# Tap tables of 32 rows, the order at the start of the second block, and the pooling gate on the unscaled input

## The chip, the cores and the metric

The kernel runs on one core of one Trainium2 chip. The metric is the device time in microseconds (us) of one execution; the median of several runs counts. A profile of one execution stands beside it. Engine names: TensorE (PE in the rows, PEld for its weight loads), VectorE (DVE), ScalarE (ACT), GpSimd (POOL) and SyncE (SP), whose queue issues most of the DMAs.

## The reference, cut to what matters

The reference runs two blocks on a sequence of 256 tokens of width 1024, in float32. The first block (a hybrid mixer, a cross attention and a large sum over 16384 experts) ends in an RMS norm. The second block has two layers, each fed by a modulated RMS norm; the first has a convolution mixer with 31 taps, the second a pooling mixer.

```python
def _rms(x, g):
    y = x * lax.rsqrt(jnp.mean(x * x, axis=-1, keepdims=True) + EPS)
    return y * g

# in each layer i of the second block
sh, sc, gt = jnp.split((silu(c) @ w_mod[i] + b_mod[i])[:, None, :], 3, axis=-1)
h = _rms(x, norm_g[i]) * (1.0 + sc) + sh
x = x + gt * o                      # o: the mixer's output for h

def _conv_mixer(h, w_in, dw, db, ln_g, ln_b, w_out):
    a, b, g = jnp.split(h @ w_in, 3, axis=-1)
    y = a * sigmoid(b)
    y = depthwise_conv(y, dw) + db          # 31 taps, centred
    return (silu(_layernorm(y, ln_g, ln_b)) * silu(g)) @ w_out

def _pool_mixer(h, w_in, w_grp, scale, w_out):
    v, g = jnp.split(h @ w_in, 2, axis=-1)
    pooled = windowed_means(v, (2, 4, 8, 16)) - v
    y = grouped_matmul(pooled, w_grp) * scale
    return (y * silu(g)) @ w_out
```

## The kernel before

Activations lie as eight slices of 128 channels by 256 tokens (`h[:, k, :]`). Every weight tile of 128 x 1024 comes from memory as `raw`, is split by ScalarE into a rounded part `hi` (line 142) and by VectorE into the rest `lo` (line 144), and is used in three matmuls for each slice (hi with the high part of the input, hi with its low part, lo with the high part). Three `raw` buffers and, in the main ring, three pairs of `hi` and `lo` are in turn; `load_next` issues the loads on SP's queue, and `take` and `split_next` run ahead of the matmuls. A tile scheduler that simulates the engines sets the final order on each engine; `issue_after(x)` in the code holds the instructions of x's engine behind x, and an order by program text decides among those that are ready.

The last stages, which the change touches:

- `peer_down` (lines 1263 to 1265) multiplies the 128 expert tiles `V` into the sums `y`. Beside it runs `second_prep`, which loads the tables of the second block: `rcnt`, `fwd`, then `ftap` and `dw` (lines 1343 to 1346, 31 rows each: one row for a tap), and `inv`, all on SP's queue between the loads of expert tiles.
- `last_pair` and `first_out` finish the first block: for each pair p of slices, VectorE adds `y` to `h`, ScalarE squares it, and TensorE adds the squares into one row sum `s2` (line 1298, two matmuls for a pair, each in two passes since the operands are plain float32).
- `second` begins with the modulated norm of the first layer. VectorE and ScalarE make `v2` and `rho` (lines 1408 to 1412), an inverse root of `s2`; `mod_input` then makes the input `xa` of the conv mixer slice by slice: `mi` = h * gain * rho on VectorE (line 1384), `xah` = mi + shift, rounded, on ScalarE (line 1386), and `xal`, what the rounding left, on VectorE (line 1387).
- The taps enter as a transfer function: `ftap` (taps by frequency) times `dw` (taps by channel) gives `wf` in eight float32 matmuls of 512 columns (line 1422, two passes each), copied out by ScalarE (line 1423). Tables m = 0 go to the PSUM pool `psM`, the six others to the four buffers of `psT`.
- `x0_gen` makes the block's own input, the first block's final norm, in `h`: a column sum `cs` on TensorE, an inverse root `r1` (lines 240 and 241 on VectorE), and eight products (line 1431).
- `natural` (lines 212 to 214) then multiplies `xa` by the weights of a and b of the conv mixer; `b_evac` joins a pair by Tanh (`th`) and a product, and goes on to the convolution by transforms.
- The output of the conv mixer is added to `h` in `out_evac`. It also makes `f`, two tiles of the gain times `h` (high and low part) with the shift of the second layer in two further columns (258 columns), while the mean square is still being summed; when it is there, line 1604 makes `r`, and line 1605 the scaled input `xa` by another `mod_input`.
- The values of the pooling mixer are made from `f` (lines 1649 to 1651), into pairs of `psT` buffers; `from_gain` then multiplies by r (VectorE) and adds the shift's column as a bias (ScalarE). The gate is made from `xa` by `pair` (lines 155 to 157), into the two buffers of `psM`, and `silu_gate` takes its Silu on ScalarE (line 1392). The pooling itself (`pooled`: adds, means, splits) is VectorE's, between the splits of the weights.
- The grouped matmuls (`mmg`, line 1680) and the product with the gate (`yg`) follow, also in `psM`, and then the output matmul.

Of the kernel before, what the change touches and what calls it, by code (L numbers as in the profile page):

```python
# [6 lines left out]
F32 = mybir.dt.float32  # L7
# [3 lines left out]
AF = mybir.ActivationFunctionType  # L11
OP = mybir.AluOpType
AX = mybir.AxisListType

T = 256
D = 1024
KB = 8
EPS = 1e-6
CW = 31
WINDOWS = (2, 4, 8, 16)  # L20
NF = 272
NC = NF // 2 - 127
# [18 lines left out]
class Net:  # L41
# [1245 lines left out]
    def first_out(self, p):  # L1287

        post, V, A, P = self.post1, self.V, self.A, self.P
        if p == 0:  # L1290
            self.s2 = self.psX.tile([128, 512], F32, tag="x", name="s2")[:, 0:T]
        hp = self.h[:, 2 * p:2 * p + 2, :]
        V.tensor_add(hp, self.y[p], hp)
        sq = post.tile([128, 2, T], F32, tag="sq2", bufs=2, name="sq2")
        A.activation(sq, hp, AF.Square)
        for i in range(2):
            k = 2 * p + i
            P.matmul(self.s2, lhsT=self.gf2[:, k, :], rhs=sq[:, i, :], start=(k == 0), stop=(k == KB - 1))
        if p == 0:
            self.sq0 = sq  # L1300
        elif p == 1:
            self.acc2 = post.tile([128, 2, T], F32, tag="rawc", name="acc2")
            V.tensor_add(self.acc2, self.sq0, sq)
        else:
            V.tensor_add(self.acc2, self.acc2, sq)
# [25 lines left out]
    def second_prep(self):  # L1331

        nc, I, pool = self.nc, self.I, self.post1
        V, A, G, P = self.V, self.A, self.G, self.P
        mod = self.mod
        xa = self.xa2 = self.newx(pool, "xa")
        self.rcnt = pool.tile([128, 4, T], F32, name="rcnt")
        nc.sync.dma_start(self.rcnt, I["rcnt"])
        yield from self.pause(8)
        f = pool.tile([128, 2, 4, 128], F32, tag="rawc", name="fwd")  # L1340
        nc.sync.dma_start(f, I["fwd"])
        yield from self.pause(8)
        self.ftap = pool.tile([CW, 4, 128], F32, name="ftap")
        nc.sync.dma_start(self.ftap, I["ftap"])
        self.dw = pool.tile([CW, D], F32, name="dw")
        nc.sync.dma_start(self.dw, I["cv_dw"])
        yield
        om = self.om = pool.tile([128, 128], F32, name="om")
        G.memset(om, 1.0 / 768)
        g2 = pool.tile([128, 8], F32, name="g2")  # L1350
        gf = self.col("norm_final", 0, 8)
        V.tensor_mul(g2, gf, gf)
        V.tensor_scalar(g2, g2, 1.0 / D, EPS / D, op0=OP.mult, op1=OP.add)
        self.gf2 = pool.tile([128, KB, 128], F32, name="gf2")
        G.tensor_copy(self.gf2, g2.unsqueeze(2).to_broadcast([128, KB, 128]))
        yield
        self.fh = pool.tile([128, 2, 4, 128], F32R, name="fh")
        self.fl = pool.tile([128, 2, 4, 128], F32R, name="fl")
        A.activation(self.fh, f, AF.Copy)
        V.tensor_sub(self.fl, f, self.fh.bitcast(F32))  # L1360
        yield
        inv = pool.tile([128, 3, T], F32, tag="rawc", name="inv")
        nc.sync.dma_start(inv, I["inv"])
        yield from self.pause(8)
        self.ih = pool.tile([128, 3, T], F32R, name="ih")
        self.il = pool.tile([128, 3, T], F32R, name="il")
        self.ln_exp(A.activation(self.ih, inv, AF.Copy))
        V.tensor_sub(self.il, inv, self.ih.bitcast(F32))
        yield
        while "mod" not in self.flags:  # L1370
            yield
        mv = mod.rearrange("p (l c) -> p l c", l=2)
        mg = self.mg = pool.tile([128, 2, 8], F32, name="mg")
        V.scalar_tensor_tensor(mg, mv[:, :, 8:16], 1.0, self.col("norm_g", 0, 16).rearrange("p (l c) -> p l c", l=2),
                               op0=OP.add, op1=OP.mult)
        V.tensor_mul(mg[:, 0, :], mg[:, 0, :], self.col("norm_final", 0, 8))
# [10 lines left out]
            i = self.V.scalar_tensor_tensor(xl[:, k, :], t, sh, xh[:, k, :].bitcast(F32), op0=OP.add, op1=OP.subtract)  # L1387
        return i

    def silu_gate(self, ps, p):  # L1390

        self.A.activation(self.sg[:, 2 * p:2 * p + 2, :], ps, AF.Silu)
        yield

    def second(self):
        nc, I, post = self.nc, self.I, self.post
        V, A, G, P = self.V, self.A, self.G, self.P
        h, mod = self.h, self.mod
        xa = self.xa2
# [4 lines left out]
        acc, s2 = self.acc2, self.s2  # L1404


        v2 = post.tile([128, T], F32, name="v2")
        V.tensor_scalar(v2, s2, EPS * EPS, None, op0=OP.add)
        rho = post.tile([128, T], F32, name="rho")
        A.activation(rho, v2, AF.Ln)  # L1410
        A.activation(rho, rho, AF.Exp, scale=-0.5)
        self.rsqrt2(post, v2, rho)
        done = self.mod_input(0, xa, rho)

        wf = [post.tile([128, 2, D], F32, tag=f"big{i}", name="wf") for i in range(2)]
        for m in range(4):
            for c in range(2):
                if m:
                    ps = self.psT.tile([128, 512], F32, tag="t", name="wfp")
                else:  # L1420
                    ps = self.psM.tile([128, 512], F32, tag="mm", name="wfm")
                P.matmul(ps, lhsT=self.ftap[:, m, :], rhs=self.dw[:, c * 512:(c + 1) * 512], start=True, stop=True)
                A.activation(wf[m // 2][:, m % 2, c * 512:(c + 1) * 512], ps, AF.Copy)

        def x0_gen():
            s1 = self.colsum(acc)
            with self.tc.issue_after(done.ins):
                v1, r1 = self.rsqrt1(post, s1, 1.0 / D, [128, T], "r1")
            self.rsqrt2(post, v1, r1)
            for k in range(KB):  # L1430
                V.scalar_tensor_tensor(h[:, k, :], h[:, k, :], self.col("norm_final", k), r1, op0=OP.mult, op1=OP.mult)
                if k % 2:
                    yield

# [121 lines left out]
        for p in range(4):  # L1556
            lg = self.pair(xa, lambda ps, p=p: gate_evac(ps, p))
# [39 lines left out]
        def out_evac(ps, p):  # L1597
            for i in range(2):
                k = 2 * p + i
                V.scalar_tensor_tensor(h[:, k, :], ps[:, i, :], mod[:, 16 + k:17 + k], h[:, k, :], op0=OP.mult, op1=OP.add)  # L1600
                A.activation(f[0][:, k, 0:T], h[:, k, :], AF.Copy, scale=gain[:, k:k + 1])
                V.scalar_tensor_tensor(f[1][:, k, 0:T], h[:, k, :], gain[:, k:k + 1], f[0][:, k, 0:T].bitcast(F32),
                                       op0=OP.mult, op1=OP.subtract)
            self.addsq(post, acc, h[:, 2 * p:2 * p + 2, :], p)
            if p == 3:
                self.r = self.rsqrt(post, self.colsum(acc), 1.0 / D, [128, T], "r")
                self.mod_input(1, xa, self.r)
            yield
        self.quad(xb, out_evac, (0, 2, 4, 6, 8))
        for p in range(2, 4):  # L1610
# [42 lines left out]
        w = [self.take(at) for _ in range(4)]  # L1653
        pss = [self.psT.tile([128, 512], F32, tag="t", name="vps")[:, 0:T + 2] for _ in range(4)]
# [6 lines left out]
        for p in range(2, 4):  # L1661
            pss = [self.psT.tile([128, 512], F32, tag="t", name="vps")[:, 0:T + 2] for _ in range(2)]
            for n in range(2):
                part(pss[n], self.take(), 0, KB)
            self.spawn(from_gain(p, pss))
            self.tick()
        for p in range(4):
            lg = self.pair(xa, lambda ps, p=p: self.silu_gate(ps, p))
        self.finish(lg)
        xo = self.newx(self.post1, "xa")  # L1670
        for q in range(2):
            hi, lo = self.take()
            for e in range(2):
                p = 2 * q + e
                ps = self.psM.tile([128, 2, T], F32, tag="mm", name="mmg")
                for db in range(2):
                    o = ps[:, db, :]
                    for k in range(2):
                        c = 512 * e + 256 * k + 128 * db
# [22 lines left out]
def layouts(np, x):  # L1702
    f = np.ascontiguousarray

    def blk(w):
        c = w.shape[1] // 128
        return w.reshape(8, 128, c, 128).transpose(2, 1, 0, 3).reshape(c, 128, 1024)
# [20 lines left out]
    for p in range(2):  # L1728
# [19 lines left out]
        "c": x["c_2"],  # L1748
        "w_mod": x["w_mod_2"].reshape(2, 1024, 24, 128).transpose(0, 2, 3, 1).reshape(48, 128, 1024),
        "cv_ab": np.stack(ab, axis=1).reshape(16, 128, 1024), "cv_g": blk(cvw[:, 2048:]),  # L1750
        "cv_dw": x["cv_dw_2"][0], "cv_out": blk(x["cv_w_out_2"][0]),
        "pl_in": blk(x["pl_w_in_2"][0]), "pl_out": blk(x["pl_w_out_2"][0]),
        "pl_grp": x["pl_w_grp_2"][0].reshape(2, 2, 2, 128, 256).transpose(0, 3, 1, 2, 4).reshape(2, 128, 1024),
    }
# [22 lines left out]
    fwd[:, 3, 0:NC] = np.sin(w * np.outer(t, fc))  # L1777
    fwd[:, 3, NC:2 * NC] = np.cos(w * np.outer(t, fc))
    lag = np.arange(CW) - CW // 2
    ftap = np.zeros((CW, 4, 128))  # L1780
    ftap[:, 0] = np.cos(w * np.outer(lag, fa))
    ftap[:, 1] = np.sin(w * np.outer(lag, fa))
    for n in range(2):
        ftap[:, 2, n * NC:(n + 1) * NC] = np.cos(w * np.outer(lag, fc))
        ftap[:, 3, n * NC:(n + 1) * NC] = np.sin(w * np.outer(lag, fc))

    inv = np.zeros((128, 3, T))
    ca = np.where(fa == 0, 0.5, 1.0)[:, None] / NF
# [26 lines left out]
```

## Time and profile before

| | us |
|---|---|
| three runs | 1341.28, 1341.85, 1340.36 |
| median | 1341.28 |
| the profiled execution | 1340.44 |
| its span | 1338.2 |
| TensorE busy in it | 1291.0 |
| VectorE busy | 988.9 |
| ScalarE busy | 643.1 |

The second block begins at about 1104 us of the span; the tap tables are loaded near 896 us. A busy engine is one that has an instruction under way; for TensorE the time of a matmul is its way through the array, so neighbours overlap, and what it delivers is seen in the number of matmuls in a stretch. The granted clock is that of TensorE, as a share of its full 2.4 GHz: it has two levels, 1.00 and 0.50 (1.2 GHz), and values between are a mean over a stretch. The mean over the whole span is 0.987. In a row of a window, the number in brackets behind a busy time counts the instructions, and the last two columns are the mean busy share of the 16 DMA engines and the GB/s that they moved.

### The profile page before, as it was taken

Reading aid. Unit: us, or ns where it says so; the run is one execution under the profiler, and the core shown is the slowest. Engines: PE = TensorE matmul, PEld = TensorE weight load, DVE = VectorE, ACT = ScalarE, POOL = GpSimd, SP = SyncE. Lnnn points to the kernel's source line nnn. Section 1 sums busy time; section 2 is a strip of 40 time slices with the busy share of each in tenths; the row PEclk is TensorE's granted clock in tenths of the full one; section 3 lists DMA queues with packets and bytes.
Section 4 is the critical chain, followed back from the end, with each engine's and each line's share of the span. In section 5 each row is a group of like instructions: output and inputs, shape, how many; then the busy total and the mean of one; then the engine's idle time right before and its main releaser. Section 6 shows DMA issues by size and latency. Waiting matters only on the chain.

```text
span 1338.2 us, 27259 instructions
## 1 busy us (share of the span) xinstructions
PE 1291.0 (96%) x11212; PEld 1262.5 (94%) x11212; DVE 988.9 (74%) x1885; ACT 643.1 (48%) x841; POOL 168.0 (13%) x175
## 2 busy tenths in 40 slices
PE   7999988999999999999999999998999998998988
PEld 7999978989999999999999999997999996998987
DVE  7897756458488837888878999985666666677884
ACT  6674335445554544343444344444444445356652
POOL 0000000002728362000000000010100000000000
PEclk9999998999999999999999999998999998998999
DMA  7644324434566667666677766676777772433553
GB/s 241 198 143 139 90 85 136 147 116 153 174 190 179 198 181 231 214 204 212 200 222 214 215 199 210 205 238 184 234 235 236 235 221 71 137 120 103 183 166 107
DMA packets 67340, 239.69 MB, mean 179 GB/s; under 512 B 8146, under 2 KB 8402, under 8 KB 67088
## 3 DMA queue, kind: packets, MB, share of 16 engines
q1 hardware_dynamic: 59536, 212.79, 52.7%
q0 software_dynamic: 7680, 25.17, 5.7%
q8 instruction: 87, 1.43, 0.4%
q14 instruction: 37, 0.30, 0.1%
HBM read 236.88 MB, written 1.05 MB: 178 GB/s over the span
## 4 chain that ended last, share of the span: by engine, by line
PE 90%; DVE 4%; ACT 2%; DMA 2%; issue 1%; SPq 0%; DVEq 0%; ACTq 0%
PE mm L155 14%; PE mm L157 14%; PE mm L156 14%; PE y L1263 9%; PE y L1265 9%; PE y L1264 9%; DVE lo L144 2%; PE mmv L212 2%; PE mm L187 2%; PE mmv L214 2%; PE mmv L213 2%; PE mm L188 2%; PE mm L186 2%; PE G L1215 1%; PE G L1216 1%; DMA raw<-in_V 1%
## 5 line engine op out<-in xcount | busy, mean ns | idle before, releaser
L142 ACT ACTIVATE hi<-raw 128x1024 fp32r<-128x1024 f32 x391 | 412.7, 1060 | 554.8 <-PE mm L156 229.0
L144 DVE TENSOR_TENSOR lo<-raw,hi 128x1024 fp32r<-128x1024 f32 x347 | 423.8, 1224 | 184.0 <-ACT hi L142 182.8
L155 PE MATMUL mm<-xbh,hi 128*128 128x256 f32 x1128 | 319.4, 283 | 0.3 <-ACT hi L142 0.3
L157 PE MATMUL mm<-xbh,lo 128*128 128x256 f32 x1128 | 316.8, 281 | 1.0 <-DVE lo L144 0.8
L156 PE MATMUL mm<-xbl,hi 128*128 128x256 f32 x1128 | 316.1, 280 | 0.0
L1263 PE MATMUL y<-xbh,hi 128*128 128x256 f32 x1008 | 285.1, 283 | 5.0 <-ACT hi L142 5.0
L1264 PE MATMUL y<-xbl,hi 128*128 128x256 f32 x1008 | 284.3, 282 | 0.0
L1265 PE MATMUL y<-xbh,lo 128*128 128x256 f32 x1008 | 283.8, 282 | 0.5 <-DVE lo L144 0.5
L157 PEld LDWEIGHTS mm<-xbh,lo 128*128 128x128 f32 x1128 | 212.2, 188 | 1.6 <-DVE lo L144 1.6
L155 PEld LDWEIGHTS mm<-xbh,hi 128*128 128x128 f32 x1128 | 212.6, 188 | 0.6 <-ACT hi L142 0.5
L156 PEld LDWEIGHTS mm<-xbl,hi 128*128 128x128 f32 x1128 | 212.6, 189 | 0.1
L1263 PEld LDWEIGHTS y<-xbh,hi 128*128 128x128 f32 x1008 | 190.9, 190 | 5.2 <-ACT hi L142 5.2
L1265 PEld LDWEIGHTS y<-xbh,lo 128*128 128x128 f32 x1008 | 190.6, 189 | 1.5 <-DVE xbl L297 0.8
L1264 PEld LDWEIGHTS y<-xbl,hi 128*128 128x128 f32 x1008 | 191.2, 190 | 0.0
L155 PE MATMUL mm<-xah,hi 128*128 128x256 f32 x448 | 128.2, 287 | 3.1 <-ACT xah L1386 3.1
L144 POOL TENSOR_TENSOR lo<-raw,hi 128x1024 fp32r<-128x1024 f32 x44 | 106.1, 2413 | 199.4 <-DVE mt L1094 123.5
L156 PE MATMUL mm<-xal,hi 128*128 128x256 f32 x448 | 128.5, 287 | 0.7 <-DVE xal L1387 0.7
L157 PE MATMUL mm<-xah,lo 128*128 128x256 f32 x448 | 128.2, 287 | 0.5 <-DVE lo L144 0.5
L1323 POOL DMA_DIRECT2D wm<-in_w_mod x96 | 51.7, 539 | 528.2 <-DVE wm L1326 512.3
L155 PEld LDWEIGHTS mm<-xah,hi 128*128 128x128 f32 x448 | 84.9, 190 | 4.3 <-ACT xah L1386 3.3
L1326 DVE SCALAR_TENSOR_TENSOR wm<-wm,silu_c 128x512 f32<-128x512 f32 x96 | 68.9, 718 | 25.0 <-DMA wm<-in_w_mod 24.6
L156 PEld LDWEIGHTS mm<-xal,hi 128*128 128x128 f32 x448 | 85.0, 190 | 2.0 <-DVE xal L1387 0.9
(463 smaller groups left out, 2181.1 us busy)
## 6 DMA issues: line engine op xcount, KB each, us to landing
raw<-in_U SPq DMA_DIRECT2D x128, 512.0 KB, 3.7
raw<-in_V SPq DMA_DIRECT2D x128, 512.0 KB, 4.2
wm<-in_w_mod POOLq DMA_DIRECT2D x96, 256.0 KB, 4.0
raw<-in_w_in SPq DMA_DIRECT2D x28, 512.0 KB, 3.7
raw<-in_cv_ab SPq DMA_DIRECT2D x16, 512.0 KB, 3.7
raw<-in_pl_in SPq DMA_DIRECT2D x16, 512.0 KB, 4.0
raw<-in_w_xk SPq DMA_DIRECT2D x8, 512.0 KB, 4.8
raw<-in_w_xv SPq DMA_DIRECT2D x8, 512.0 KB, 4.2
```

What stands on the lines that cost most here:

```text
L142: self.A.activation(hi, raw, AF.Copy)
L144: i = (self.G if self.order[m][1] else self.V).tensor_sub(lo, raw, hi.bitcast(F32))
L155: self.P.matmul(ps, lhsT=hi[:, w], rhs=xh[:, k, :], start=(k == 0 and first), stop=False, skip_group_check=True)
L156: self.P.matmul(ps, lhsT=hi[:, w], rhs=xl[:, k, :], start=False, stop=False, skip_group_check=True)
L157: self.last_mm = self.P.matmul(ps, lhsT=lo[:, w], rhs=xh[:, k, :], start=False, stop=(k == KB - 1), skip_group_check=True)
L186: self.P.matmul(o, lhsT=hi[:, c], rhs=xh[:, k, :], start=a, stop=False, skip_group_check=True)
L187: self.P.matmul(o, lhsT=hi[:, c], rhs=xl[:, k, :], start=False, stop=False, skip_group_check=True)
L1263: P.matmul(o, lhsT=hi[:, w], rhs=wh[:, s, :], start=(j == 0 and db % 2 == 0), stop=False, skip_group_check=True)
L1264: P.matmul(o, lhsT=hi[:, w], rhs=wl[:, s, :], start=False, stop=False, skip_group_check=True)
L1265: P.matmul(o, lhsT=lo[:, w], rhs=wh[:, s, :], start=False, stop=(j == 127), skip_group_check=True)
L1323: nc.gpsimd.dma_start(w, self.I["w_mod"][n, :, 512 * c:512 * (c + 1)])
L1326: V.scalar_tensor_tensor(w, w, 1.0, s, op0=OP.mult, op1=OP.mult, accum_out=part[:, n, c:c + 1])
```

## The change

It does three things.

1. The tap tables `ftap` and `dw` get 32 rows in place of 31; the added row is zero in both.
2. At the start of the second block: v2, rho and `mod_input` get high priority; the six tap matmuls of m = 1 to 3 are held behind the last matmul of `s2` on TensorE, their copies behind the Exp of rho on ScalarE; the VectorE steps of `x0_gen` (the inverse root's two and the eight products) are held behind the last xal.
3. In the pooling mixer the second `mod_input` is gone. The gate is multiplied from `f`, as the values are, by the same `part`, into `psT`; the new `gate_out` copies the shift's column (VectorE), multiplies by r (VectorE) and takes the Silu with that column as bias (ScalarE), slice by slice.

```diff
+CP = 32
@@ first_out
-            P.matmul(self.s2, lhsT=self.gf2[:, k, :], rhs=sq[:, i, :], start=(k == 0), stop=(k == KB - 1))
+            self.last_s = P.matmul(self.s2, lhsT=self.gf2[:, k, :], rhs=sq[:, i, :], start=(k == 0), stop=(k == KB - 1))
@@ second_prep
-        self.ftap = pool.tile([CW, 4, 128], F32, name="ftap")
+        self.ftap = pool.tile([CP, 4, 128], F32, name="ftap")
         nc.sync.dma_start(self.ftap, I["ftap"])
-        self.dw = pool.tile([CW, D], F32, name="dw")
+        self.dw = pool.tile([CP, D], F32, name="dw")
@@ second
-        V.tensor_scalar(v2, s2, EPS * EPS, None, op0=OP.add)
-        A.activation(rho, v2, AF.Ln)
-        A.activation(rho, rho, AF.Exp, scale=-0.5)
-        self.rsqrt2(post, v2, rho)
-        done = self.mod_input(0, xa, rho)
+        with self.tc.high_priority():
+            V.tensor_scalar(v2, s2, EPS * EPS, None, op0=OP.add)
+            A.activation(rho, v2, AF.Ln)
+            made = A.activation(rho, rho, AF.Exp, scale=-0.5)
+            self.rsqrt2(post, v2, rho)
+            done = self.mod_input(0, xa, rho)
...
-                P.matmul(ps, lhsT=self.ftap[:, m, :], rhs=self.dw[:, c * 512:(c + 1) * 512], start=True, stop=True)
-                A.activation(wf[m // 2][:, m % 2, c * 512:(c + 1) * 512], ps, AF.Copy)
+                with self.tc.issue_after(self.last_s.ins) if m else nullcontext():
+                    P.matmul(ps, lhsT=self.ftap[:, m, :], rhs=self.dw[:, c * 512:(c + 1) * 512], start=True, stop=True)
+                with self.tc.issue_after(made.ins) if m else nullcontext():
+                    A.activation(wf[m // 2][:, m % 2, c * 512:(c + 1) * 512], ps, AF.Copy)
...
                 v1, r1 = self.rsqrt1(post, s1, 1.0 / D, [128, T], "r1")
-            self.rsqrt2(post, v1, r1)
+                self.rsqrt2(post, v1, r1)
             for k in range(KB):
-                V.scalar_tensor_tensor(h[:, k, :], h[:, k, :], self.col("norm_final", k), r1, op0=OP.mult, op1=OP.mult)
+                with self.tc.issue_after(done.ins):
+                    V.scalar_tensor_tensor(h[:, k, :], h[:, k, :], self.col("norm_final", k), r1, op0=OP.mult, op1=OP.mult)
...
                 self.r = self.rsqrt(post, self.colsum(acc), 1.0 / D, [128, T], "r")
-                self.mod_input(1, xa, self.r)
...
+        def gate_out(p, pss):
+            t = post.tile([128, 2, T], F32, tag="t2", name="gt")
+            b = post.tile([128, 2], F32, tag="gb", bufs=2, name="gb")
+            for i in range(2):
+                V.tensor_copy(b[:, i:i + 1], pss[i][:, T:T + 1])
+                V.tensor_mul(t[:, i, :], pss[i][:, 0:T], self.r)
+                A.activation(self.sg[:, 2 * p + i, :], t[:, i, :], AF.Silu, bias=b[:, i:i + 1])
+            yield
         for p in range(4):
-            lg = self.pair(xa, lambda ps, p=p: self.silu_gate(ps, p))
+            pss = [self.psT.tile([128, 512], F32, tag="t", name="gps")[:, 0:T + 2] for _ in range(2)]
+            for n in range(2):
+                part(pss[n], self.take(), 0, KB)
+                self.tick()
+            lg = self.spawn(gate_out(p, pss))
+            self.tick()
```

`silu_gate` is taken out, and `layouts` fills the added row of both tables with zeros.

## Rows read from the trace of the kernel before

**Rows 1.** The page's part 4: the chain that ended last, shares of the span.

```profile
PE 90%; DVE 4%; ACT 2%; DMA 2%; issue 1%; SPq 0%; DVEq 0%; ACTq 0%
```

**Rows 2.** Windows: stretch, length, busy us of PE, PEld, DVE, ACT, POOL, clock, DMA.

```profile
925.00:1104.00 179.00, 179.00 (x1528) 179.00 (x1527) 116.67 (x161) 82.96 (x95) 16.28 (x33) 1.00 0.77 233
...
1140.00:1215.00 75.00, 75.00 (x623) 74.19 (x623) 50.52 (x64) 37.65 (x52) 3.41 (x4) 1.00 0.44 133
```

**Rows 3.** The same view of two stretches behind the loads of the tables.

```profile
909.00:915.50 6.50, 1.21 (x4) 0.92 (x5) 1.70 (x2) 2.22 (x3) 0.00 (x0) 0.84 0.07 29
...
908.60:922.10 13.50, 8.06 (x37) 6.75 (x35) 6.78 (x9) 7.29 (x8) 0.54 (x1) 0.75 0.31 93
```

**Rows 4.** DMA issues of the whole span: count, KB each, median us to landing.

```profile
dw<-in_cv_dw SPq DMA_DIRECT2D x1, 124.0 KB
cols<-in_cols SPq DMA_DIRECT2D x1, 102.5 KB, 2.1
```

**Rows 5.** The loads of expert tiles (line 113) issued from 885 to 925 us.

```profile
DMA to landing us min/median/max: 3.6/4.4/15.3
```

**Rows 6.** Waits of ScalarE, 896 to 925 us: total, times, longest.

```profile
ACT hi L142 <- DMA raw<-in_V: 9.4, 1, 9.4
```

**Rows 7.** Chain of waits, 1104 to 1120 us: start, us, engine, tile, line, count.

```profile
1105.60 1.92 PE s L1298 x8
1107.53 3.63 PE wfp L1422 x8
1111.15 3.41 PE s L1298 x8
...
1115.76 1.06 PE cs L268 x4
...
1119.71 0.58 PE mmv L212
```

**Rows 8.** Windows, columns as in rows 2, at the second block's start.

```profile
1107.50:1111.10 3.60, 3.60 (x10) 1.38 (x9) 1.41 (x3) 2.42 (x4) 0.00 (x0) 1.00 0.83 269
1111.40:1114.80 3.40, 3.40 (x9) 2.30 (x8) 0.20 (x1) 0.39 (x1) 0.00 (x0) 0.50 0.01 5
...
1118.30:1125.00 6.70, 5.29 (x23) 5.15 (x24) 6.33 (x17) 3.24 (x9) 0.00 (x0) 0.50 0.00 0
```

**Rows 9.** Timeline of VectorE there: start, us, line, operation, tiles, idle before.

```profile
1114.60 0.42 DVE L1408 TENSOR_SCALAR v<-s 128x256 f32<-128x256 f32 x1 [5.59 <-PE s L1298]
...
1118.11 0.88 DVE L1384 SCALAR_TENSOR_TENSOR mi<-h,mg,rho 128x256 f32<-128x256 f32 x2
...
1130.79 0.48 DVE L1387 SCALAR_TENSOR_TENSOR xal<-mi,mod,xah 128x256 fp32r<-128x256 f32 x1
```

**Rows 10.** Timeline of TensorE: the first matmul behind the first gated pair.

```profile
1136.18 0.38 PE L212 MATMUL mmv<-hi,xah 128*128 128x256 f32 x1 [1.53 <-ACT th L1449]
```

**Rows 11.** VectorE's groups, 1257 to 1304 us: count, busy us, mean ns, idle before.

```profile
L1384 DVE SCALAR_TENSOR_TENSOR mi<-h,mg,rr 128x256 f32<-128x256 f32 x8 | 3.7, 479 | 0.0
L1387 DVE SCALAR_TENSOR_TENSOR xal<-mi,mod,xah 128x256 fp32r<-128x256 f32 x8 | 3.6, 479 | 0.0
L1642 DVE TENSOR_TENSOR vt<-vps,rr 128x256 f32<-128x256 f32 x8 | 3.2, 417 | 0.0
...
L1641 DVE COPY vb<-vps 128x1 f32<-128x1 f32 x8 | 1.2, 154 | 0.2 <-PE vps L1651 0.2
```

**Rows 12.** Waits of TensorE, 1258 to 1311 us: total, times, longest.

```profile
PE mm L155 <- ACT xah L1386: 3.1, 1, 3.1
...
PE mmg L1680 <- ACT sg L1392: 1.0, 1, 1.0
PE mm L156 <- DVE xal L1387: 0.7, 1, 0.7
```

**Rows 13.** Busy time by stretch, columns as in rows 2, in the pooling mixer.

```profile
1277.80:1282.50 4.70, 4.68 (x24) 4.41 (x24) 4.70 (x10) 1.52 (x4) 0.16 (x2) 0.64 0.62 216
...
1258.00:1283.30 25.30, 20.84 (x155) 19.91 (x153) 25.13 (x52) 15.55 (x27) 0.30 (x4) 0.93 0.56 167
```

More of the change, by code (lines that the diff above doesn't have):

```diff
@@ L1388, in mod_input @@
         return i
-    def silu_gate(self, ps, p):
-        self.A.activation(self.sg[:, 2 * p:2 * p + 2, :], ps, AF.Silu)
-        yield
     def second(self):
@@ L1750, in layouts @@
         "cv_ab": np.stack(ab, axis=1).reshape(16, 128, 1024), "cv_g": blk(cvw[:, 2048:]),
-        "cv_dw": x["cv_dw_2"][0], "cv_out": blk(x["cv_w_out_2"][0]),
+        "cv_dw": np.concatenate([x["cv_dw_2"][0], np.zeros((CP - CW, 1024), x["cv_dw_2"].dtype)]), "cv_out": blk(x["cv_w_out_2"][0]),
         "pl_in": blk(x["pl_w_in_2"][0]), "pl_out": blk(x["pl_w_out_2"][0]),
@@ L1779, in layouts @@
     lag = np.arange(CW) - CW // 2
-    ftap = np.zeros((CW, 4, 128))
-    ftap[:, 0] = np.cos(w * np.outer(lag, fa))
-    ftap[:, 1] = np.sin(w * np.outer(lag, fa))
+    ftap = np.zeros((CP, 4, 128))
+    ftap[:CW, 0] = np.cos(w * np.outer(lag, fa))
+    ftap[:CW, 1] = np.sin(w * np.outer(lag, fa))
     for n in range(2):
-        ftap[:, 2, n * NC:(n + 1) * NC] = np.cos(w * np.outer(lag, fc))
-        ftap[:, 3, n * NC:(n + 1) * NC] = np.sin(w * np.outer(lag, fc))
+        ftap[:CW, 2, n * NC:(n + 1) * NC] = np.cos(w * np.outer(lag, fc))
+        ftap[:CW, 3, n * NC:(n + 1) * NC] = np.sin(w * np.outer(lag, fc))
     inv = np.zeros((128, 3, T))
```

## The prediction

> **What bounds the kernel now.** I read the chain that ended last first: TensorE holds 90% of it, so this kernel is as long as TensorE's work plus what TensorE loses [rows 1]. Then I read the table by stage, to see where it loses. From 925 to 1104 us and from 1140 to 1215 us it is busy all the time at full clock [rows 2]. Two things follow. A step that is only moved inside such a stretch gains nothing; and whatever is won ahead of such a stretch stays won, because nothing else in it is waiting to take the place of TensorE. So the change has to be costed in the three places where it touches a loss: 908 to 922 us (the tap tables arrive), 1104 to 1136 us (the second block begins) and 1258 to 1304 us (the pooling mixer). One full-rate matmul of 256 columns costs 179 us / 1528 = 0.117 us [rows 2].
>
> **Part A, tap tables of 32 rows.** The arithmetic is the same (row 31 is zero), and a tap matmul streams the same 512 columns, so on TensorE this is worth nothing. What differs is the transfer. The tables are two DMAs of 31 rows on SP's queue ahead of the expert tiles; `dw`, the larger, has 124 KB [rows 4]. Between 909.0 and 915.5 us the DMA engines together are 0.07 busy and move 29 GB/s [rows 3]: of 16 engines that is one (1/16 is 0.0625). One engine is still working off a queue that the other 15 have finished. One `raw` tile took 15.3 us to land where the median of ten is 4.4 [rows 5], and ScalarE, which splits it, waited 9.4 us for it [rows 6]. TensorE ran dry. From 908.6 to 922.1 us it did 37 matmuls at a mean clock of 0.75 [rows 3]; 35 of them at 0.117 and two tap passes at 0.45 (a pass is 3.63/8 us, [rows 7]) are 5.0 us of work in 13.5 us. If the tables spread over the engines, the stall and the low clock behind it go, and 13.5 - 5.0 = **8.5 us** are won. Behind it 179 us at full use follow, so all of it reaches the end.
>
> The trace shows no transfer of 32 rows, so this is bounded from both sides. If 32 rows go the way of 31, the gain is 0. If they go the way of a 128-row transfer of like size (102.5 KB of `cols`, landed in 2.1 us, [rows 4]), it is 8.5. I take 8.5: what sets the 31-row transfer apart is not its size but that 31 rows can't be dealt out evenly over 16 engines, and 32 can. A loss has no source here, as a row of zeros adds 124/31 = 4 KB to the larger table.
>
> The Trainium skill states the rule (DMA: Bandwidth & Descriptors, section "Why a DMA increments its semaphore by 16 and not by 1"): a DMA uses the largest number of engines up to 16 that divides its slowest dimension, so 127 partitions go on one engine and 96 on sixteen; 31 would be one and 32 sixteen. The 0.07 above agrees for 31; no row shows 32.
>
> **Part B, the order at the start of the second block.** Before, TensorE took eight passes of the tap matmuls ahead of the last eight passes of the sum `s2` [rows 7], and everything that follows needs `s2`: VectorE's v2 starts at 1114.60 only [rows 9], and the first input matmul at 1119.71 [rows 7]. Now the six later tap matmuls (12 passes) stand behind the sum on TensorE, their copies behind the Exp of rho on ScalarE, and the ten VectorE steps of `x0_gen` behind the last xal on VectorE. No DMA moves, and SP's and GpSimd's queues are not passed by anything.
>
> Worked out: the first half of the sums ends at 1107.53; the second half takes another 1.92 us, so s2 is done at 1109.45 instead of 1114.56, 5.1 us earlier [rows 7]. From there to the first input took 5.15 us (1119.71 - 1114.56), with tap copies in between; at most that again gives 1114.6. TensorE meanwhile has its taps, 12 x 0.45 = 5.4 us, to 1114.85, and the column sum, 1.06 us, to 1115.9. So the chain is hidden by work that must be done anyway, and TensorE becomes the bound. Its whole list from 1105.60 to the end of the first gated pair is 3.84 (sums) + 5.4 + 1.06 + 96 x 0.117 = 11.2 (inputs), together 21.5 us: 1127.1. Before, that pair ended at 1136.18 - 1.53 = 1134.65 [rows 10]. The ceiling of B is **7.5 us**. VectorE keeps up: before, its last xal started at 1130.79, 16.2 us after v2 [rows 9], with ten `x0_gen` steps in between; its first mi came 3.5 us after v2 (1118.11 - 1114.60), so sixteen steps of 0.48 us [rows 11] end near 1109.6 + 3.5 + 7.7 = 1120.8. TensorE wants the last at 1115.9 + (24 + 9) x 0.117 = 1119.8 (one pass over four slices, then three more), so up to 1.0 us is lost; the steps overlap a little in the trace, and I take none. The `x0_gen` steps now end near 1125 (ten more of 0.48 us at most); nothing reads their result before the conv mixer's output is added. The wait of 1.53 us on `th` at 1136 stays.
>
> The clock takes part of it back. TensorE was busy 3.60 of 3.60 us with almost nothing but taps and had full clock, then the granted clock was 0.50 (1.2 GHz) for 3.4 us although TensorE never paused; during those it ran the 128-row sums and the clock came back; later it was 0.50 for 6.7 us, after taps and a pause [rows 8]. The new order puts 5.4 us of taps in one piece, so I expect one fall while they run. Priced by the longer of the two rows it costs half of 6.7, 3.4 us; two falls as before cost 5.1, none costs 0. I take one long one: B = 7.5 - 3.4 = **4.1 us**, with 7.5 - 5.1 - 1.0 = 1.4 and 7.5 as the ends. A loss is excluded by the list above: with both falls it still ends earlier than before.
>
> The Trainium skill's rule on this (TensorE: Matmul & The Clock Gate, Part 1) is that the clock follows how busy TensorE has been. By it, taps without a pause would keep 2.4 GHz; the row of 1111.4 us speaks against it for matmuls of 31 rows. I weigh it below as a rival.
>
> **Part C, the gate of the pooling mixer.** The old gate needed `xa`, the scaled input: eight mi and eight xal on VectorE at 0.48 us each and eight xah on ScalarE. VectorE was busy 25.13 of 25.3 us there [rows 13], so each of these stood in line with the splits, and TensorE waited: 3.1 us for xah, 0.7 for xal, and 1.0 for the Silu that frees a PSUM buffer for `mmg` [rows 12]. Between them it ran 24 matmuls in 4.7 us at a mean clock of 0.64 [rows 13], where 24 x 0.117 is 2.8: 1.9 lost. Together 3.1 + 0.7 + 1.0 + 1.9 = 6.7 us, all owed to operands that the new gate doesn't read: `f` is there already for the values. On VectorE, 16 x 0.48 = 7.7 us go; eight copies (0.15) and eight products (0.42), 4.6 us [rows 11], come, but later, with the gates. ScalarE loses eight xah and does eight Silu of 256 in place of four of 512: about even, and it isn't the bound. The matmuls have 258 columns in place of 256, 192 x 0.001 = 0.2 us.
>
> The new wait is on PSUM: a gate pair's two buffers come free when VectorE has done its products, not when ScalarE has done the Silu. Four buffers hold two pairs, and a pair takes 48 x 0.117 = 5.6 us, so the products have one pair's time of slack. Behind them in VectorE's order stand the splits and the pooling, for which TensorE waits in turn. I take **6.3 us** (6.7 less 0.4), with 3.1 (VectorE's own relief, 7.7 - 4.6) and 7 as the ends.
>
> **Sum.** 8.5 + 4.1 + 6.3 = 18.9 us. The profiled execution took 1340.44 us (span 1338.2), 0.84 below the median of 1341.28; the sum is of that execution and I take it off both: 1321.5 for its like, **1322.4** for the median.
>
> **The rivals.**
> 1. *The clock stays up behind the sums* (the skill's rule). B is 7.5: 1341.28 - 22.3 = 1319.0. For it: the 128-row sums now stand closer together ahead of the taps. Against: the fall at 1111.4 with no pause. Chance 0.12.
> 2. *VectorE stays the bound in the mixer.* Its queue is nearly full in [rows 13], and the gate's products now sit in it, so TensorE waits for buffers where it waited for xah; C is 1 and, with two falls of the clock, B is 2.4: 1341.28 - 11.9 = 1329.4. Chance 0.15.
> 3. *32 rows still go on one engine.* A is 0: 1341.28 - 10.4 = 1330.9. Against it is the arithmetic of 16. Chance 0.05.
> 4. *Slower.* Place: the four gate pairs. If VectorE's order puts a pair's products behind the pooling of a window (four adds at 0.7, two products and a split, also 0.7) and two splits at 1.22, that is some 7 us beyond the matmuls, and with no buffer left each pair waits. Four such waits are 28 us: 1341.3 - 18.9 + 28 = 1350. It decides from (18.9 + 2.7) / 4 = 5.4 us per pair on. Against it: the slack of 5.6 us. Chance 0.04.
>
> **How the numbers follow.** Forecast (A, B and C near their values): 0.61, by itself 1318 to 1328. Rivals as above, 0.36 together; 0.03 is left for mixtures that come out even. The range 1316 to 1331 takes in A at 8.5 with B and C at both ends (1341.28 - 8.5 - 7.5 - 7 = 1318.3, and 1341.28 - 8.5 - 1.4 - 3.1 = 1328.3), rivals 1 to 3, and 2 us below for the pauses of the middle stretch, whose clock falls may shift. A measurement of this kernel can tell about 0.2%, 2.7 us, from no change. Faster 0.93, same 0.03, slower 0.04.
>
> **What would show it.** A: no stretch near 910 us with DMA at 0.06, `dw` and `ftap` landing in a few us, TensorE without a pause there and no fall of the clock. B: the eight last passes of the sums ahead of all later taps, v2 some 5 us earlier relative to the end of `y`, the first input within 12 us of that end (15 before), no xal waited for. C: no wait on xah, xal or sg; products of the gate within 5.6 us of their matmuls. Wrong it would be if the low DMA share is still there, if the clock falls twice in B, or if a new wait on the gate's products of over 1 us shows in the mixer.

## The result and the profile after

| | before | after |
|---|---|---|
| median, us | 1340.82 (1339.30 to 1341.85, 4 runs) | 1319.76 (1317.54 to 1322.94, 4 runs) |
| the profiled execution, us | 1340.44 | 1318.12 |
| its span, us | 1338.2 | 1316.4 |
| mean granted clock in it | 0.987 | 0.994 |

The ratio is 0.9846, with a 95% interval of 0.9831 to 0.9861: 21 us, or 1.5%, faster. The forecast was 1322.4, 2.6 us more than was measured.

In the program after, lines from 20 on have moved down by one, those of the second block a little differently: the load is L114, the splits L143 (hi) and L145 (lo), the sum `s` L1299, v2 L1406, the taps L1420 and the input matmuls L213 to L215. (In the program before, `r` of the pooling mixer is made in line 1606 and its scaled input `xa` in line 1607.) First the page's part 4 of the kernel after, the chain that ended last, against [rows 1]:

```profile
PE 95%; DVE 3%; ACT 1%; issue 1%; DMA 0%; SPq 0%; DVEq 0%; ACTq 0%
```

TensorE's share went from 90% to 95%; DMA's 2% went to 0. Next the windows of the kernel after (columns as in [rows 2]), the DMA issues, and the landing of the expert tiles issued from 885 to 925 us:

```profile
880.00:925.00 45.00, 45.00 (x406) 43.81 (x405) 31.88 (x49) 21.76 (x25) 4.46 (x8) 1.00 0.78 242
...
1101.10:1107.70 6.60, 6.60 (x17) 2.74 (x16) 5.15 (x12) 5.39 (x13) 0.00 (x0) 1.00 0.21 85
1107.70:1120.70 13.00, 11.54 (x97) 11.12 (x96) 11.22 (x23) 8.43 (x14) 0.00 (x0) 1.00 0.18 55
...
1257.00:1280.00 23.00, 23.00 (x195) 23.00 (x194) 21.73 (x40) 15.08 (x21) 0.16 (x2) 1.00 0.66 204
1280.00:1288.50 8.50, 6.44 (x50) 5.81 (x49) 8.18 (x16) 4.62 (x7) 0.00 (x0) 1.00 0.67 207
```

```profile
dw<-in_cv_dw SPq DMA_DIRECT2D x1, 128.0 KB, 7.0
...
ftap<-in_ftap SPq DMA_DIRECT2D x1, 64.0 KB, 7.0
```

```profile
DMA to landing us min/median/max: 3.5/4.7/7.3
```

The first window is where [rows 3] had 6.5 us with 1.21 us of work: now TensorE is busy 45.00 of 45 us at full clock. The latest expert tile takes 7.3 us in place of 15.3 [rows 5].

The chain of waits at the start of the second block (start, us, engine, tile, line, count), against [rows 7]:

```profile
1096.32 1.05 PE wfm L1420 x2
1097.37 3.83 PE s L1299 x16
1101.19 2.78 PE wfp L1420 x6
```

The sixteen passes of the sum now stand in one piece, and they start 8.2 us earlier than the first of them did before (1105.60 - 1097.37): that is part A. Then VectorE and TensorE in the timeline (start, us, engine, line, operation, tiles, idle before):

```profile
1101.23 0.42 DVE L1406 TENSOR_SCALAR v<-s 128x256 f32<-128x256 f32 x1 [0.45 <-PE s L1299]
...
1111.29 0.48 DVE L1388 SCALAR_TENSOR_TENSOR xal<-mi,mod,xah 128x256 fp32r<-128x256 f32 x1 [0.18 <-ACT xah L1387]
...
1112.61 3.26 DVE L1431 SCALAR_TENSOR_TENSOR h<-h,cols,rr 128x256 f32<-128x256 f32 x8
1115.79 2.35 DVE L145 TENSOR_TENSOR lo<-raw,hi 128x1024 fp32r<-128x1024 f32 x2
```

```profile
1107.72 0.38 PE L213 MATMUL mmv<-hi,xah 128*128 128x256 f32 x1
...
1120.72 0.39 PE L213 MATMUL mmv<-hi,xah 128*128 128x256 f32 x1 [0.69 <-ACT th L1449]
```

v2 starts 3.9 us behind the start of the sums (9.0 before: 1114.60 - 1105.60); the first input matmul 10.4 us (14.1 before). What stood at 1136.18 [rows 10] stands at 1120.72, 15.5 us earlier: 8.2 of part A and 7.2 of part B. The rest of the 21.8 us of the span, 6.3, comes behind that point, from the pooling mixer. There TensorE works through all gate pairs without a pause (23.00 of 23.00 us in the window from 1257), and this is what is left of its waits from 1236 to 1290 us (total, times, longest), in place of [rows 12]:

```profile
PE mmg L1694 <- DVE xbl L291: 1.3, 1, 1.3
PE mm L187 <- DVE yg L1699: 0.5, 1, 0.5
PE mmg L1693 <- DVE yg L1699: 0.3, 1, 0.3
```

### The profile page after: what moved, and what is told of

It reads as the page before. It is cut to its first block, busy times and chain, and to the rows that moved or that the text cites. A ratio compares the mean times of both kernels' runs of the same rounds, so it can differ in the third digit from the quotient of the medians.

```text
span 1316.4 us, 27266 instructions
## 1 busy us (share of the span) xinstructions
PE 1281.6 (97%) x11212; PEld 1255.9 (95%) x11212; DVE 985.4 (75%) x1885; ACT 640.5 (49%) x837; POOL 168.0 (13%) x175
## 4 chain that ended last, share of the span: by engine, by line
PE 95%; DVE 3%; ACT 1%; issue 1%; DMA 0%; SPq 0%; DVEq 0%; ACTq 0%
PE mm L158 14%; PE mm L156 14%; PE mm L157 14%; PE y L1264 9%; PE y L1265 9%; PE y L1266 9%; PE mm L188 2%; PE mm L189 2%; PE mm L187 2%; PE mmv L213 2%; PE mmv L214 2%; PE mmv L215 1%; PE G L1216 1%; PE G L1217 1%; DVE lo L145 1%; PE py L791 1%
## 5 line engine op out<-in xcount | busy, mean ns | idle before, releaser
L143 ACT ACTIVATE hi<-raw 128x1024 fp32r<-128x1024 f32 x391 | 412.8, 1060 | 541.4 <-PE mm L157 224.6
L145 DVE TENSOR_TENSOR lo<-raw,hi 128x1024 fp32r<-128x1024 f32 x347 | 423.5, 1224 | 171.7 <-ACT hi L143 170.9
L145 POOL TENSOR_TENSOR lo<-raw,hi 128x1024 fp32r<-128x1024 f32 x44 | 106.1, 2413 | 198.7 <-DVE mt L1095 122.9
L158 PE MATMUL mm<-xah,lo 128*128 128x256 f32 x384 | 109.7, 286 | 0.4 <-DVE lo L145 0.4
L156 PE MATMUL mm<-xah,hi 128*128 128x256 f32 x384 | 110.0, 287 | 0.0
L157 PE MATMUL mm<-xal,hi 128*128 128x256 f32 x384 | 109.8, 286 | 0.0
L158 PEld LDWEIGHTS mm<-xah,lo 128*128 128x128 f32 x384 | 72.3, 188 | 1.7 <-issue 1.0
L157 PEld LDWEIGHTS mm<-xal,hi 128*128 128x128 f32 x384 | 72.4, 189 | 0.9 <-issue 0.7
```

What stands on the lines that cost most here:

```text
L143: self.A.activation(hi, raw, AF.Copy)
L145: i = (self.G if self.order[m][1] else self.V).tensor_sub(lo, raw, hi.bitcast(F32))
L156: self.P.matmul(ps, lhsT=hi[:, w], rhs=xh[:, k, :], start=(k == 0 and first), stop=False, skip_group_check=True)
L157: self.P.matmul(ps, lhsT=hi[:, w], rhs=xl[:, k, :], start=False, stop=False, skip_group_check=True)
L158: self.last_mm = self.P.matmul(ps, lhsT=lo[:, w], rhs=xh[:, k, :], start=False, stop=(k == KB - 1), skip_group_check=True)
```

## The experiments

### One part at a time

Each of the first three kernels takes over one part of the change and leaves the rest as before.

`e1_rows32`, part A alone:

```diff
+CP = 32
...
-        self.ftap = pool.tile([CW, 4, 128], F32, name="ftap")
+        self.ftap = pool.tile([CP, 4, 128], F32, name="ftap")
...
-        self.dw = pool.tile([CW, D], F32, name="dw")
+        self.dw = pool.tile([CP, D], F32, name="dw")
```

> The kernel before with tables of 32 rows and nothing else. Theory (one DMA engine carried the 31 rows): the stall near 910 us and the low clock behind it go, 8.2 us faster as the shift of the end of y showed in the changed kernel (1104.55 to 1096.32), ratio 0.9939; the later stages keep their waits (3.1 us on xah in the mixer). Rival (the stall came from the order of the second block's work, or from the size of the loads): stall and time as before, ratio 1.000. On the clock behind the sums: if 32 rows are what kept it up in the changed kernel, it doesn't fall during the taps here either, and 1.7 us more are won (ratio 0.9926); if the new order did it, it falls as before.

Measured: 1332.79 us against 1340.62, 7.8 less (ratio 0.9942, 0.9925 to 0.9960). In its windows the stretch of [rows 3] is whole. The second block waits for xah as before, 1.8 us, and the clock falls there once, so nothing of B came with it:

```profile
909.00:915.50 6.50, 6.50 (x49) 5.61 (x48) 4.84 (x7) 4.64 (x6) 0.54 (x1) 1.00 0.74 241
...
1111.20:1117.90 6.70, 5.31 (x24) 5.18 (x25) 6.33 (x17) 3.24 (x9) 0.00 (x0) 0.50 0.00 0
```

```profile
PE mmv L213 <- ACT xah L1387: 1.8, 1, 1.8
```

In this execution the sums start at 1100.12, only 5.5 us earlier than before: the matmuls of `y` ran at the slower of two paces, which the part on the clock comes back to.

`e2_order`, part B alone, with 31 rows (`CP = 31`, and the gate as before):

> The kernel before with the new order at the start of the second block alone, tables of 31 rows. Theory of the prediction (taps in one piece let the clock fall once): 4.1 us faster, ratio 0.997, a stretch at 0.50 of 3.4 to 6.8 us behind the sums. Rival (the order itself keeps the clock up, as in the changed kernel): 7.2 us faster, ratio 0.9946, no fall there. The stall near 910 us stays as before in both.

Measured: 1333.39 us, 7.2 less by the medians (ratio 0.9956, 0.9938 to 0.9974). Four of its six executions took 1331.7 to 1333.8 us, the two others 1337.4 and 1337.6, at the lowest mean clocks (0.988 and 0.987). Its windows, behind the loads of the tables and at the start of the second block:

```profile
909.00:915.50 6.50, 1.61 (x6) 1.32 (x7) 2.00 (x3) 2.60 (x4) 0.00 (x0) 0.72 0.06 25
1110.00:1130.00 20.00, 18.55 (x127) 15.03 (x127) 17.43 (x34) 14.44 (x25) 0.00 (x0) 1.00 0.23 69
```

The stall is still there with DMA at 0.06, and the clock stays at 1.00 through the taps in this execution, although they have 31 rows.

`e3_gate`, part C alone, with 31 rows and the old order:

> The kernel before with the gate of the pooling mixer from the unscaled input alone. Theory: the waits on xah, xal and sg go, 6.8 us faster as the shift of the last stage showed in the changed kernel, ratio 0.9949, with a wait of mmg on the last window's split of about 1.3 us in their place. Rival (the gain there came from the earlier start of the stage, with weights loaded further ahead): under 3 us faster, ratio above 0.998, and waits of TensorE on the gate's products.

Measured: 1334.57 us, 6.05 less (ratio 0.9950, 0.9932 to 0.9968). TensorE is busy nearly all of the stretch of the gate, and the one new wait is the one that the kernel after has too:

```profile
1257.00:1295.00 38.00, 37.88 (x314) 37.63 (x313) 34.99 (x66) 25.64 (x37) 0.31 (x4) 1.00 0.58 173
```

```profile
PE mmg L1690 <- DVE xbl L291: 1.3, 1, 1.3
```

Three parts, 7.8 + 7.2 + 6.05 = 21.1 us; the whole, 21.1 as well (each part by its interval to some 2.4 us). They lie in three losses that are far apart, and within these intervals what is won in one is kept in the others.

### Part A: is it the number of rows?

`e4_mm31`: the tables keep 32 rows, the matmuls read 31 of them. `e5_rows37` and `e6_rows34`: tables of 37 and of 34 rows, the added ones zero.

```diff
-                    P.matmul(ps, lhsT=self.ftap[:, m, :], rhs=self.dw[:, c * 512:(c + 1) * 512], start=True, stop=True)
+                    P.matmul(ps, lhsT=self.ftap[:CW, m, :], rhs=self.dw[:CW, c * 512:(c + 1) * 512], start=True, stop=True)
```

```diff
-CP = 32
+CP = 37
```

> The changed kernel with tables of 32 rows transferred, but the tap matmuls take the first 31 rows. Theory A (the rows matter for the transfer alone): time as the changed kernel, 21 us below before (ratio 0.9846), no stall near 910 us. On the clock: if a 32nd row in the matmul is what kept it up behind the sums, it falls here, for 3.4 us or more, and the time is 1.7 to 3.4 us above the changed kernel (ratio 0.986 to 0.987); if the order did it, there is no fall.

> The changed kernel with tables of 37 rows (six zero rows). Theory (rows that can't be dealt out evenly go on one engine, and 37 is prime): the stall near 910 us is back, with the DMA engines at 0.06 for 37/31 of the time, TensorE idle for 6 us or more, the clock at 0.50 behind it, and a span some 10 us above the changed kernel's 1316.4. Rival (tables of fewer than 32 rows are the slow ones): no stall, a span of 1313 to 1321 us.

> The changed kernel with tables of 34 rows (2 x 17). Theory: two engines carry them, 17 rows of 6 KB each instead of 31 on one: the DMA share in the tail near 0.12, about half as long as before; the tile behind lands some 3 to 4 us earlier than with 31, so TensorE waits 0 to 2 us there and the clock holds; span 1314 to 1322. Rival (anything that isn't 16 engines is one): as with 37 rows, a wait of 5 us or more. Rival (32 rows and more are all alike): tables landed in 7.0 us, no tail.

`e4_mm31` took 1319.59 us, as the kernel after, and has no stall: what counts is the transfer, not the matmuls. With 37 rows one execution took 1329.78 us, with 34 rows 1326.85. The windows from 910 us, of 37 rows and then of 34:

```profile
910.00:912.00 2.00, 0.00 (x0) 0.00 (x0) 0.00 (x0) 0.00 (x0) 0.00 (x0) 1.00 0.06 25
```

```profile
910.00:912.00 2.00, 1.11 (x7) 0.90 (x8) 1.83 (x2) 1.12 (x3) 0.00 (x0) 1.00 0.13 53
```

The DMA share is 0.06 with 37 rows (one of 16 engines) and 0.13 with 34 (two), at 25 and 53 GB/s; with 32 rows no such stretch is left. The latest expert tile lands after 17.0, 11.2 and 7.3 us in this order:

```profile
DMA to landing us min/median/max: 3.5/4.3/17.0
```

```profile
DMA to landing us min/median/max: 3.6/4.2/11.2
```

TensorE waits 6.7 us for a split with 37 rows and 1.4 with 34, and the sums start at 1105.8 and 1100.4 us in place of 1097.4: the stall costs some 8.4 and 3.0 us. More rows and more bytes than 32, and yet slower: it is the number of rows, by whether it can be dealt out. The Trainium skill's rule (DMA: Bandwidth & Descriptors, "Why a DMA increments its semaphore by 16 and not by 1"), the largest number of engines up to 16 that divides the slowest dimension, gives 1 for 31 and 37, 2 for 34 and 16 for 32; the shares of 0.07, 0.06 and 0.13 agree. Both executions lost more than their stalls: their clocks also fell in the second block, for 10.2 us each. So the span with 34 rows, 1325.1 us, lies above the 1314 to 1322 that were expected. The fall is the next question.

### Part B: which hold does the work, and what does the clock do?

`e7_nox0hold` drops the hold on the ten VectorE steps of `x0_gen`, so that they stand as in the kernel before; `e8_notaphold` drops the holds on the taps and their copies.

```diff
-                self.rsqrt2(post, v1, r1)
+            self.rsqrt2(post, v1, r1)
...
-                with self.tc.issue_after(done.ins):
-                    V.scalar_tensor_tensor(h[:, k, :], h[:, k, :], self.col("norm_final", k), r1, op0=OP.mult, op1=OP.mult)
+                V.scalar_tensor_tensor(h[:, k, :], h[:, k, :], self.col("norm_final", k), r1, op0=OP.mult, op1=OP.mult)
```

```diff
-                with self.tc.issue_after(self.last_s.ins) if m else nullcontext():
+                with nullcontext():
...
-                with self.tc.issue_after(made.ins) if m else nullcontext():
+                with nullcontext():
```

> The changed kernel without the hold on the ten VectorE steps of the block's own input. Theory: they come between the xal steps again, the last xal starts some 3 us later, TensorE waits 1 to 3 us for xal and 0.8 us less for a lo; time 0 to 3 us above the changed kernel. Rival (the high priority of mod_input is enough): the same order of xal and the same time.

> The changed kernel without the holds on the tap matmuls and their copies. Theory: eight tap passes go ahead of the last eight of the sum again, s2 is 3.6 us later, TensorE waits about 2 us for the first input, 3 to 5 us above the changed kernel. Rival (the high priority alone brings the order): the same time as the changed kernel, 1320 us.

`e7_nox0hold`: 1319.76 us (1319.00 to 1320.18), the same as with the hold. Without the hold, most of xal still stands ahead of the products; only the last two come late, among them, and TensorE waits for neither. But its clock was at 0.50 there, so it wanted them later than at full clock; whether it would have waited for them then, no trace shows. Timeline of its VectorE, and a window:

```profile
1110.74 2.85 DVE L1430 SCALAR_TENSOR_TENSOR h<-h,cols,rr 128x256 f32<-128x256 f32 x7
...
1113.91 0.48 DVE L1388 SCALAR_TENSOR_TENSOR xal<-mi,mod,xah 128x256 fp32r<-128x256 f32 x1
...
1114.70 0.47 DVE L1388 SCALAR_TENSOR_TENSOR xal<-mi,mod,xah 128x256 fp32r<-128x256 f32 x1
```

```profile
1103.80:1113.90 10.10, 10.10 (x27) 5.97 (x26) 9.17 (x23) 6.27 (x15) 0.00 (x0) 0.50 0.00 0
```

`e8_notaphold`: 1321.82 us (1320.65 to 1328.29), 2.1 more. Eight passes of taps stand ahead of the last sums again, and TensorE waits for xah as before the change; behind this wait its clock fell. The chain, TensorE's wait, and a window:

```profile
1097.43 1.93 PE s L1299 x8
1099.36 3.62 PE wfp L1420 x8
1102.98 1.93 PE s L1299 x8
```

```profile
PE mmv L213 <- ACT xah L1387: 1.8, 1, 1.8
```

```profile
1111.40:1114.70 3.30, 3.24 (x15) 2.94 (x15) 2.94 (x8) 1.63 (x4) 0.00 (x0) 0.50 0.00 0
```

By the medians the hold on the taps is worth 2.1 us, but the two intervals overlap (0.9848 to 0.9907, and 0.9831 to 0.9861 for the kernel after), so the times alone don't show it. The trace does: the first input comes 12.5 us behind the start of the sums (1109.91 - 1097.43), in place of 10.4. That is less than the 3.6 us that the eight passes last, since they only change places with other work of TensorE. The hold on `x0_gen` carries nothing that can be measured. What is left of B would then be the high priority's. No run dropped that, so this is argued and not shown.

The clock: in the profiled executions of the kernel after and of `e2_order` it stays at 1.00 behind the sums. In those of `e4_mm31` and `e7_nox0hold`, and of 37 and 34 rows, it does not, although TensorE has the same order there up to the first inputs (in `e4_mm31` throughout). Nor is it a matter of 31 or 32 rows in the taps: `e2_order` has 31 and no fall, `e7_nox0hold` 32 and a fall. `e4_mm31`, the sums, three stretches from the taps on, and the first matmul behind the first gated pair:

```profile
1097.00 3.82 PE s L1299 x16
```

```profile
1101.00:1103.50 2.50, 2.50 (x7) 1.03 (x7) 1.50 (x4) 1.91 (x4) 0.00 (x0) 1.00 0.48 187
1103.60:1113.70 10.10, 10.10 (x23) 5.23 (x23) 8.13 (x18) 7.04 (x16) 0.00 (x0) 0.50 0.00 0
1113.80:1120.00 6.20, 6.20 (x57) 6.20 (x56) 4.44 (x10) 2.13 (x2) 0.00 (x0) 1.00 0.08 17
```

```profile
1124.08 0.39 PE L213 MATMUL mmv<-hi,xah 128*128 128x256 f32 x1 [0.69 <-ACT th L1449]
```

TensorE is busy before the fall and through it, 2.50 of 2.50 and 10.10 of 10.10 us, and runs at 1.2 GHz for some 10 us. The next pair starts at 1124.08 in place of 1120.72, though its sums began 0.4 us earlier (1097.00 against 1097.37): such a fall costs 3.7 us here, less than half of its 10.2 us, in part because TensorE then has no wait of 0.8 us for a split.

`e9_rows128` asks whether the fall comes from taps that fill few rows of TensorE: the tables get all 128 rows, cleared by GpSimd, and the transfers still bring 32. The clearing comes with a step of waiting ahead of the loads of the tables (`pause(8)`). `e10_again` is the kernel after, on the same chip.

```diff
+        self.ftap = pool.tile([128, 4, 128], F32, name="ftap")
+        self.dw = pool.tile([128, D], F32, name="dw")
+        G.memset(self.ftap, 0.0)
+        G.memset(self.dw, 0.0)
+        yield from self.pause(8)
...
-        nc.sync.dma_start(self.ftap, I["ftap"])
+        nc.sync.dma_start(self.ftap[0:CP], I["ftap"])
...
-        nc.sync.dma_start(self.dw, I["cv_dw"])
+        nc.sync.dma_start(self.dw[0:CP], I["cv_dw"])
```

> The changed kernel with the two tap tables widened to all 128 rows: GpSimd clears them early, the transfers still bring 32 rows. Passes and columns of the tap matmuls stay the same, so without the clock this is worth nothing; what changes is how many rows of TensorE the taps use. Theory 1, the clock fall behind the sums comes from the taps' few rows: with 128 rows the granted clock stays at 1.00 from 1097 to 1120 us in the profiled execution, the low stretches left are the two near 203 and 1206 us, the mean clock of the executions is 0.994 or above in nearly all, and the time is 1 to 3 us below that of the changed kernel on the same chip (1316.5 to 1319). Theory 2, the fall does not ask for rows and comes in some executions of any such order: the mean clock varies from 0.990 to 0.995 as before, the time is within 1.5 us of the changed kernel's. Theory 3, the clearing on GpSimd holds up the transfers on SP's queue or the modulation's loads: a wait of TensorE near 890 to 920 us, up to 3 us longer.

> The changed kernel itself, once more, on the chip of the widened tables: 1318 to 1322 us. Theory that the fall behind the sums comes in some executions only: in this profiled execution it may be there (a low stretch of 7 to 10 us near 1104) or not, with the same program; the mean clocks of the executions spread over 0.990 to 0.995 and the times follow them, 0.001 of the mean clock for some 2.6 us (a stretch at half clock of length d lowers the mean by 0.5 d / 1317 and costs d / 2 where TensorE is the bound). Rival, that the fall is a matter of the order: it is absent in every execution, and the clocks agree within 0.001.

With 128 rows: 1319.53 us (1317.61 to 1321.63, five runs), mean clocks 0.994 to 0.996. The kernel after: 1321.34 (1320.48 to 1322.10, five runs), 0.992 to 0.994. The ratios to before overlap (0.9828 to 0.9855 and 0.9837 to 0.9864). Both profiled executions keep the clock behind the sums (the one with 128 rows is shown):

```profile
1101.10:1120.70 19.60, 18.01 (x121) 14.84 (x120) 16.57 (x34) 14.66 (x26) 0.00 (x0) 1.00 0.27 85
```

This doesn't settle which theory holds. Theory 1 asked for 1 to 3 us and for clocks of 0.994 and more, and got 1.8 us and just that; but the 1.8 us lie within what the two intervals allow, and a row of one execution without a fall is no evidence when the kernel with 32 rows shows the same. Theory 3 is out: TensorE has no wait from 880 to 930 us. Against the expectation, the times of `e10_again` don't follow the mean clock either (0.994 goes with 1320.48 as well as with 1321.34).

A second cause of scatter stands in the traces. The kernel after and `e10_again` are one program, and neither profiled execution has the fall behind the sums, yet they took 1318.12 and 1321.34 us. Here are both in the same stretch of `y`, the kernel after first, and behind them a late fall that `e10_again` alone has:

```profile
930.00:1090.00 160.00, 160.00 (x1366) 160.00 (x1365) 104.56 (x145) 74.52 (x84) 15.07 (x31) 1.00 0.77 236
```

```profile
930.00:1090.00 160.00, 160.00 (x1351) 160.00 (x1350) 104.24 (x145) 73.93 (x84) 15.20 (x31) 1.00 0.76 234
...
1289.60:1292.90 3.30, 3.27 (x16) 3.00 (x15) 3.10 (x7) 2.10 (x3) 0.00 (x0) 0.50 0.38 150
```

TensorE is busy throughout at full clock, and does 15 matmuls fewer: one takes 118.4 ns (160 / 1351) in place of 117.1. So the sums of `e10_again` start at 1100.30 us in place of 1097.37, 2.9 us later; 0.3 of it is a wait for a split near 906 us. Of the twelve profiled executions, `e1_rows32`, `e3_gate`, `e9_rows128` and `e10_again` have the slower pace (1350 or 1351 matmuls in this window) and the eight others the faster (1366). What sets the pace stays open. A difference of 2 us and more between two single executions can come from it alone; the kernels before and after have the same pace in their profiles, so the 8.2, 7.2 and 6.3 us are free of it.

## Why the prediction was right

**Part A**, 8.5 forecast: 8.2 us by the start of the sums, 7.8 by `e1_rows32`. The step, a stall and a low clock that both go if the tables spread over the engines, held. The choice between the ends of 0 and 8.5 was right too, though its price was not: I took the near row of `cols`, 2.1 us to landing, and `dw` took 7.0. That cost nothing, as the expert tiles still came in time. The 0.3 us between 8.5 and 8.2 fit no row.

**Part B**, 4.1 forecast: 7.2 in the profile, and by the medians of `e2_order` too. The mechanism held step by step: v2 5.1 us earlier relative to the start of the sums, and no xal waited for. The first input came 11.4 us behind the end of `y` (1107.72 - 1096.32), within the 12 named. The term that was mis-sized is the clock. I read two falls in [rows 8] as owed to taps, and took one as all but certain, at 3.4 us. The price was near, as `e4_mm31` showed (3.7); the certainty was not right. In the profiled executions of the kernel after, `e2_order`, `e9_rows128` and `e10_again` there is none; in `e4_mm31`, `e5_rows37`, `e6_rows34` and `e7_nox0hold` there is one. A term of 3.4 us at about even odds would have given some 5.8 for B and 1320.7 in all. Rival 1, the clock stays up (1319.0, chance 0.12), was nearer to the median than the forecast (0.8 us off against 2.6), and came true in the profiled execution. Its reason did not: by the Trainium skill (TensorE: Matmul & The Clock Gate, Part 1) the clock follows how busy TensorE has been, and `e4_mm31` shows it fall at a TensorE that was busy all the time.

Two small terms were wrong and cancelled. The wait on `th` that "stays" fell from 1.53 to 0.69 us. In its place came a wait of 0.8 us for a lo split: the ten steps of `x0_gen`, held behind the last xal, stand on VectorE ahead of that split (1112.61, then 1115.79). I had named who reads their result, but not what is queued behind them.

**Part C**, 6.3 forecast: 6.3 us in the profile, 6.05 by `e3_gate`. No wait on xah, xal or sg is left, and the clock stays up through the gate. That the number came out so well is luck in part. The forecast took 0.4 us for what is new, and 2.1 came (1.3, 0.5 and 0.3). Against that, two waits of before stand in the view of [rows 12] and were not in the sum:

```profile
PE mm L186 <- DVE yg L1686: 1.4, 1, 1.4
...
PE vps L1651 <- DVE lo L144: 0.6, 1, 0.6
```

With them it is 6.7 + 2.0 - 2.1 = 6.6 us. The new wait was looked for in the wrong place: not at the gate's products, which keep up (TensorE has no pause up to the end of the last gate matmul at 1280.15), but at the last window's pooling, whose split `xbl` comes behind products and splits on VectorE. It costs 1.3 us, and 0.3 and 0.5 beside it. Timelines of VectorE and of TensorE:

```profile
1280.51 0.42 DVE L1672 TENSOR_TENSOR gt<-gps,rr 128x256 f32<-128x256 f32 x1
...
1282.64 1.21 DVE L145 TENSOR_TENSOR lo<-raw,hi 128x1024 fp32r<-128x1024 f32 x1
1283.77 0.87 DVE L1699 SCALAR_TENSOR_TENSOR yg<-mmg,cols,sg 128x256 f32<-128x256 f32 x2
1284.55 1.22 DVE L145 TENSOR_TENSOR lo<-raw,hi 128x1024 fp32r<-128x1024 f32 x1
1285.69 0.69 DVE L291 TENSOR_TENSOR xbl<-m,xbh 128x512 fp32r<-128x512 f32 x1
```

```profile
1286.43 0.38 PE L1694 MATMUL mmg<-xbl,hi 128*128 128x256 f32 x1 [1.29 <-DVE xbl L291]
```

Rival 2 (VectorE stays the bound) had the right engine and a price that was too high; rivals 3 and 4 didn't come.

The sum, 18.9 us, missed 2.2 us by the medians and 2.9 by the spans of the two profiled executions. In the profiles the fall that 3.4 us were taken off for didn't come, and A and B (against its ceiling of 7.5) were each 0.3 us short. Left open: what sets whether the clock falls behind the sums, and whether one and the same program shows both cases. The kernel after has two profiled executions (`e10_again` is the second), both without the fall; one of its others, 1321.41 us, had a mean clock of 0.991 where the rest of that set had 0.994, and the four of `e4_mm31` spread from 0.990 to 0.996. Falls of that length in some executions of one program would fit this, but a mean clock doesn't say where they were. Not tried: a kernel without the high priority, and an order that takes the last window's split ahead of the weights' splits.

## What to carry to other kernels

Look for stretches in which the mean DMA share is about 1/16 while an engine waits: a transfer whose rows can't be dealt out over the engines may be holding up what is queued behind it, and a padding row can be worth as much as a new order (7.8 and 7.2 us here, not told apart). Where a kernel is bound by one engine, cost a change by the places where that engine waits; three parts in three such places added up to the whole. Before you put a few us between two executions down to an edit, compare the number of matmuls in a stretch that neither edit touches. When you hold work back, look up what stands behind it on the same engine, not only who reads its result.

## What the runs showed that was not expected

With the same order of instructions on TensorE, and TensorE busy throughout, the granted clock went to 0.50 for 10.1 us at the taps in some profiled executions and stayed at 1.00 in others. A table of 34 rows has more bytes than one of 32 and moved at 53 GB/s over two DMA engines; one of 37 rows moved at 25 GB/s over one. And at full clock, without a wait, one program did 1366 matmuls in 160 us in one execution and 1351 in another.
